# Rotary embedding on one core: the first tile loaded in pieces of two, two and four rows, the sine table spread in a PSUM bank of its own, the last tile stored whole

## The chip, the core and the metric

The kernel runs on one core of a Trainium2 chip. The metric is the device time of one execution in microseconds (us); where several runs are given, it is their median. The engines of the core are TensorE (PE in the profile; PEld are its weight loads), VectorE (DVE), ScalarE (ACT), GpSimd (POOL) and SyncE (SP), which issues all transfers here. Sixteen DMA engines move the data between HBM (the chip's large memory) and SBUF (the core's working memory). PSUM is the small memory into which TensorE writes.

## The reference

`x` has 16 batches of 512 positions of 1024 float32 values, that is 16 heads of 64. Each head is cut into two halves of 32, which are rotated with a cosine and a sine of the position:

```
x = x.reshape(batch, seq, num_heads, head_dim)
x1, x2 = x[..., :half_dim], x[..., half_dim:]
cos, sin = cos[None, :, None, :], sin[None, :, None, :]      # 512 x 32 each
rotated = concatenate([x1 * cos - x2 * sin, x1 * sin + x2 * cos], axis=-1)
```

33.55 MB are read and as many are written.

## The kernel before

**Tiles.** Eight tiles `xt` are worked on in turn. A tile holds two batches: each of its 128 partitions has eight consecutive positions ("rows" 0 to 7 of 1024 values, 32 KB together), so a tile has 4 MB. Five buffers (`BUFS`) hold tiles; results are written over the input in the same buffer, and stored from there. Tiles 5, 6 and 7 use the buffers of tiles 0, 1 and 2 again, so their loads wait until the stores of those have landed.

**Order.** The order is written out by hand (`manual_schedule`), and each engine executes its instructions in the program's order. All transfers are issued by SyncE, one behind the other, and run on one queue: the first piece of tile 0 (`FIRST`, rows 0 to 2), the two tables, the rest of tile 0, tiles 1 to 4, four dummy requests of a few rows of the sine table into `spare` (`EXTRA`, L92), which nobody reads, then the stores of tiles 0, 1, 2, the loads of tiles 5, 6, 7 and the stores of tiles 3 to 7. The last tile is stored in two halves (`LAST_OUT`): rows 0 to 3 once they are done, rows 4 to 7 at the end. Each transfer takes the next of eight completion counters in turn, and the issue of a transfer also waits until the one before it on its counter has landed.

**Tables.** The tables come in as 64 partitions. Two matmuls with a 0/1 matrix `spread` copy them to 128 partitions in PSUM: sine at L113, cosine at L114, both into the bank `tab`. VectorE then writes the sine with both signs to SBUF (`sns`: L116, L117) and copies the signs of row 0 back to `tab` as `own_t` (L119), into the place where the sine was.

**Work on a tile.** The rows are treated in three ways:

- Rows 1-2, 4-5 and 6-7 (`PAIRS`): VectorE multiplies a pair by the cosine into the PSUM buffer `pd` (four banks, L141), GpSimd multiplies the swapped halves by the signed sine into an SBUF buffer `b` (L165), VectorE adds the two into `xt` (L189).
- Row 3: GpSimd makes the sine product, VectorE the cosine product into `pe_ps`, TensorE adds the one onto the other (L176), ScalarE copies the sum to `xt` (L181).
- Row 0: VectorE makes both products (`own_ps` at L141, L150), TensorE adds them (L176), ScalarE copies (L209).

Row 0 of the first tile can begin when its piece and the cosine are there; the first product of GpSimd needs `sns` and rows 1 and 2.

Of the kernel before, what the change touches and what calls it, by code (L numbers as in the profile page):

```python
# [8 lines left out]
FP32 = mybir.dt.float32  # L9
# [9 lines left out]

PAIRS = ((1, 2), (4, 5), (6, 7))  # L20

FIRST = (3, 8)
LAST_OUT = (4, 8)

EXTRA = (2, 4, 5, 6)


@with_exitstack
def kernel(
# [14 lines left out]
    P = nc.NUM_PARTITIONS  # L44
    batch, seq, dim = x.shape
    nh = num_heads
    hd = dim // nh
    half = hd // 2
    PB = P // NB
    KK = seq // PB  # L50
# [13 lines left out]
    pd = ctx.enter_context(tc.tile_pool(name="pd", bufs=1, space=bass.MemoryType.PSUM))  # L64
# [5 lines left out]
    def load(t, lo=0, hi=KK):  # L70
        if tiles[t] is None:
            tiles[t] = xp.tile([P, F], FP32, name="xt")
        s = slice(lo * dim, hi * dim)
        nc.sync.dma_start(out=tiles[t][:, s], in_=x_v[t][:, s])  # L74

    def store(t, lo=0, hi=KK):
        s = slice(lo * dim, hi * dim)
        nc.sync.dma_start(out=out_v[t][:, s], in_=tiles[t][:, s])

    load(0, 0, FIRST[0])  # L80
    tabs = bp.tile([P, 2 * dim], FP32, name="b")
# [3 lines left out]
    nc.sync.dma_start(out=cos_sb, in_=cos_v)  # L85
    for lo, hi in zip(FIRST, FIRST[1:]):
        load(0, lo, hi)
    for t in range(1, BUFS):
        load(t)
    spare = fixed.tile([16, len(EXTRA), 16], FP32)  # L90
    for i, n in enumerate(EXTRA):
        nc.sync.dma_start(out=spare[:n, i], in_=sin_v[:n, :16])  # L92
# [10 lines left out]
    sns = fixed.tile([P, KK, 2, half], FP32)  # L103
    tab = pfix.tile([P, BANK], FP32)
    cos_t = tab[:, : KK * half]
    sin_t = tab[:, KK * half : 2 * KK * half]
    spread = fixed.tile([PB, P], FP32)
    eye = ident[:PB, :PB]
    nc.vector.tensor_copy(
# [81 lines left out]
    def stores(t):  # L191
        lo = 0
        for hi in LAST_OUT if t == NT - 1 else (KK,):
            store(t, lo, hi)
# [64 lines left out]
```

## Time and profile before

| | |
|---|---|
| median of 6 runs | 162.67 us (162.26 to 162.93) |
| the profiled execution | 162.85 us, of which the span of the engines' work is 161.1 |
| VectorE busy | 136.3 us (85% of the span) |
| GpSimd busy | 127.1 us (79%) |
| TensorE busy | 58.2 us (36%) |
| ScalarE busy | 18.7 us (12%) |
| transfers | 67.25 MB, mean 418 GB/s |

The profile is of one execution. Shares are averages over the span, so stretches of it are looked at one by one: slices of a fortieth of the span, in which a digit is the busy share in tenths, or stretches given in microseconds. `L165` is line 165 of the kernel. A row of the timeline has start, duration, engine, line, operation, output and input, and in brackets how long the engine stood idle before it, and who released it. For a transfer the profile gives the line, the size and the time from issue to landing.

### The profile page before, as it was taken

Reading aid. Unit: us, or ns where it says so; the run is one execution under the profiler, and the core shown is the slowest. Engines: PE = TensorE matmul, PEld = TensorE weight load, DVE = VectorE, ACT = ScalarE, POOL = GpSimd, SP = SyncE. Lnnn points to the kernel's source line nnn. Section 1 sums busy time; section 2 is a strip of 40 time slices with the busy share of each in tenths; the row PEclk is TensorE's granted clock in tenths of the full one; section 3 lists DMA queues with packets and bytes.
Section 4 is the critical chain, followed back from the end, with each engine's and each line's share of the span. In section 5 each row is a group of like instructions: output and inputs, shape, how many; then the busy total and the mean of one; then the engine's idle time right before and its main releaser. Section 6 shows DMA issues by size and latency. Waiting matters only on the chain.

```text
span 161.1 us, 443 instructions
## 1 busy us (share of the span) xinstructions
PE 58.2 (36%) x71; PEld 18.1 (11%) x71; DVE 136.3 (85%) x85; ACT 18.7 (12%) x25; POOL 127.1 (79%) x38
## 2 busy tenths in 40 slices
PE   3132805066404840293109330753057303930000
PEld 0111201021002200130004000300021002200000
DVE  1069969999999999999999999999999999997000
ACT  0002401003100301021100310031003100210000
POOL 1049999999999999988998899989989899830000
PEclk9999965557755585559555855576556855595555
DMA  5999999999999999999999999999999999999993
GB/s 189 397 437 441 439 472 391 399 513 391 399 513 391 391 456 456 391 439 472 393 423 480 391 431 480 391 415 488 399 399 505 399 399 496 407 399 444 415 431 142
DMA packets 2787, 67.25 MB, mean 418 GB/s; under 512 B 354, under 2 KB 482, under 8 KB 482
## 3 DMA queue, kind: packets, MB, share of 16 engines
q1 hardware_dynamic: 2786, 67.24, 97.6%
q14 instruction: 1, 0.01, 0.0%
HBM read 33.69 MB, written 33.55 MB: 417 GB/s over the span
## 4 chain that ended last, share of the span: by engine, by line
DVE 68%; issue 12%; POOL 6%; DMA 4%; PE 1%; SPq 0%; DVEq 0%
DVE xt L189 33%; DVE pd L141 31%; POOL b L165 6%; DMA b<-in_sin_dram 4%; DVE pe_ps L141 3%; PE tab L113 1%; PE tab L114 1%; DVE sns L116 0%; DVE xt L150 0%; DVE own_ps L141 0%; SPq L74 0%; DVE sns L117 0%; DVEq L189 0%
## 5 line engine op out<-in xcount | busy, mean ns | idle before, releaser
L165 POOL TENSOR_TENSOR b<-xt,sns 128x2048 f32<-128x2048 f32 (+1 forms) x32 | 126.4, 3981 | 14.5 <-DVE sns L117 9.0
L189 DVE TENSOR_TENSOR xt<-pd,b 128x2048 f32<-128x2048 f32 x24 | 54.9, 2287 | 2.4 <-POOL b L165 1.6
L141 DVE TENSOR_TENSOR pd<-xt,tab 128x2048 f32<-128x2048 f32 x24 | 55.0, 2291 | 0.2
L176 PE MATMUL own_ps<-xt,ident 128*128 128x512 f32 x32 | 29.8, 1086 | 57.0 <-DVE xt L150 51.3
L176 PE MATMUL pe_ps<-b,ident 128*128 128x512 f32 x32 | 26.5, 926 | 23.5 <-DVE pe_ps L141 23.5
L176 PEld LDWEIGHTS own_ps<-xt,ident 128*128 128x128 f32 x32 | 9.4, 323 | 75.3 <-DVE xt L150 60.5
L209 ACT COPY xt<-own_ps 128x1024 f32<-128x1024 f32 x8 | 8.1, 1013 | 75.9 <-PE own_ps L176 75.9
L181 ACT COPY xt<-pe_ps 128x512 f32<-128x512 f32 x16 | 9.4, 587 | 35.6 <-PE pe_ps L176 35.6
L176 PEld LDWEIGHTS pe_ps<-b,ident 128*128 128x128 f32 x32 | 7.3, 249 | 43.1 <-DVE pe_ps L141 34.7
L141 DVE TENSOR_TENSOR pe_ps<-xt,tab 128x512 f32<-128x512 f32 x16 | 11.0, 686 | 0.0
L141 DVE TENSOR_TENSOR own_ps<-xt,tab 128x1024 f32<-128x1024 f32 x8 | 9.8, 1224 | 0.0
L150 DVE TENSOR_TENSOR xt<-xt,tab 128x1024 f32<-128x1024 f32 x8 | 9.7, 1214 | 0.0
L116 DVE TENSOR_SCALAR sns<-tab 128x256 f32<-128x256 f32 x1 | 0.4, 424 | 8.0 <-PE tab L114 8.0
L209 ACT ACT_TABLE_LOAD x1 | 1.3, 1283 | 15.2 <-DVE xt L150 15.2
L113 PE MATMUL tab<-b,spread 64*128 64x256 f32 x2 | 1.2, 696 | 4.8 <-DMA b<-in_sin_dram 4.8
L101 PE MATMUL own_ps<-zero 128*128 128x512 bf16 x2 | 1.0, 622 | 1.2 <-DVE zero L97 1.2
L113 PEld LDWEIGHTS tab<-b,spread 64*128 64x128 f32 x2 | 0.5, 306 | 5.7 <-issue 5.7
L114 PE MATMUL tab<-b,spread 64*128 64x256 f32 x2 | 1.1, 631 | 0.0
L97 DVE MEMSET zero<- 128x256 uint32 x1 | 0.3, 272 | 0.9 <-PEq L240 0.9
L114 PEld LDWEIGHTS tab<-b,spread 64*128 64x128 f32 x2 | 0.7, 333 | 0.2
L101 PE MATMUL pe_ps<-zero 128*128 128x512 bf16 x1 | 0.6, 634 | 0.0
L101 PEld LDWEIGHTS <-zero 128*128 128x128 bf16 x3 | 0.3, 125 | 1.5 <-DVE zero L97 1.2
(9 smaller groups left out, 1.8 us busy)
## 6 DMA issues: line engine op xcount, KB each, us to landing
xt<-in_x_dram SPq DMA_DIRECT2D x7, 4096.0 KB, 29.5
out_dram<-xt SPq DMA_DIRECT2D x7, 4096.0 KB, 24.8
out_dram<-xt SPq DMA_DIRECT2D x2, 2048.0 KB, 11.1
xt<-in_x_dram SPq DMA_DIRECT2D x1, 2560.0 KB
xt<-in_x_dram SPq DMA_DIRECT2D x1, 1536.0 KB
b<-in_sin_dram SPq DMA_DIRECT2D x1, 64.0 KB
b<-in_cos_dram SPq DMA_DIRECT2D x1, 64.0 KB
spare<-in_sin_dram SPq DMA_DIRECT2D x1, 0.1 KB
```

The costliest lines, as they stand in the source:

```text
L97: nc.vector.memset(zero, 0.0)
L101: nc.tensor.matmul(out=ps, lhsT=zero[:, :P], rhs=zero, start=True, stop=True)
L113: nc.tensor.matmul(out=sin_t, lhsT=spread, rhs=sin_sb, start=True, stop=True)
L114: nc.tensor.matmul(out=cos_t, lhsT=spread, rhs=cos_sb, start=True, stop=True)
L116: nc.vector.tensor_scalar_mul(out=sns[:, :, 0, :], in0=sin_k, scalar1=-1.0)
L141: nc.vector.tensor_tensor(out=o, in0=i, in1=cb, op=ALU.mult)
L150: nc.vector.tensor_tensor(out=heads(r), in0=heads(r), in1=s, op=ALU.mult)
L165: nc.gpsimd.tensor_tensor(out=o, in0=i, in1=sb, op=ALU.mult)
L176: nc.tensor.matmul(out=ps, lhsT=ident, rhs=other, start=False, stop=True, skip_group_check=True)
L181: nc.scalar.copy(out=r, in_=pe_ps)
L189: nc.vector.tensor_tensor(out=r, in0=ps, in1=b, op=ALU.add)
L209: nc.scalar.copy(out=r0, in_=own_ps)
```

## The change

Tile 0 is loaded in three pieces (rows 0-1, then behind the tables rows 2-3 and rows 4-7). The last tile is stored in one transfer, behind its last sum. The four dummy requests have one row each. The spread sine goes into the first bank of the `pd` buffer, so that `tab` holds the cosine and `own_t` alone. The instructions of TensorE, ScalarE, GpSimd and VectorE are the same in kind, number and order; SyncE issues one load more and one store less.

```diff
-FIRST = (3, 8)
-LAST_OUT = (4, 8)
-
-EXTRA = (2, 4, 5, 6)
+FIRST = (2, 4, 8)
+LAST_OUT = (8,)
+
+EXTRA = (1, 1, 1, 1)
...
     tab = pfix.tile([P, BANK], FP32)
     cos_t = tab[:, : KK * half]
-    sin_t = tab[:, KK * half : 2 * KK * half]
+    sin_t = pd.tile([P, 2 * dim], FP32, name="pd")[:, : KK * half]
```

## The prediction

> **What bounds the kernel now.** I read the page's 40 slices first, then the table of stretches, the chain, the DMA issues, the waits, and last the single DMA packets of the trace. The slices:
>
> ```profile
> DVE  1069969999999999999999999999999999997000
> ...
> DMA  5999999999999999999999999999999999999993
> ```
>
> A slice is 4.03 us. VectorE (DVE) is full until slice 36 and then stops; the DMA engines are full from slice 1 to slice 38 and go on after VectorE has ended. The stretches say it in numbers:
>
> ```profile
> core 0: us, PE busy (x) PEld busy (x) DVE busy (x) ACT busy (x) POOL busy (x), PEclk, DMA share, GB/s
> ...
> 8.00:148.00 140.00, 56.22 (x68) 17.35 (x66) 135.77 (x83) 18.68 (x25) 126.43 (x32) 0.63 1.01 433
> 148.00:158.50 10.50, 0.00 (x0) 0.00 (x0) 0.00 (x1) 0.00 (x0) 0.00 (x0) 0.50 0.93 399
> ```
>
> The column before the last is the DMA engines' busy share: 1.01 for 140 us (packets overlap a little), at 433 GB/s, and no compute engine works after 148.0. The chain of waits names VectorE for 68%, but it follows one chain only and can't show that the transfers had no idle time either:
>
> ```profile
> DVE 68%; issue 12%; POOL 6%; DMA 4%; PE 1%; SPq 0%; DVEq 0%
> ```
>
> So two resources run full side by side. Which one sets the end is read from the packets. I put them into 16 chains, one per DMA engine (each packet begins within about 30 ns of another's end). In each chain all transfers lie in the order of issue, back to back, from 2.0-2.8 us on: a 32 KB packet takes 1.213 us, a 16 KB one 0.611, so about 9 ns per packet are fixed. Fifteen chains end at 158.54 to 159.15, one at 160.14, and the span ends 0.93 later, at 161.07. Tile 6's store leaves the chains at 148.81 to 149.40, and at 150.41 in the late one. The last half store, issued at 148.0, starts moving only at 153.7, when the half before it is through. VectorE's end at 148.0 is therefore early by over 5 us; **the DMA engines are the bound**, and their work is 67.24 MB plus losses (busy time per engine 157.2 of 161.1 us).
>
> The late chain: at 80.1 a packet of the instruction queue takes its engine for 0.31 us, the next packet is 0.40 too long, and at the change from loads to stores near 109 it loses 0.56, as the last one still loading. The profile page has that packet as its second queue:
>
> ```profile
> q1 hardware_dynamic: 2786, 67.24, 97.6%
> q14 instruction: 1, 0.01, 0.0%
> ```
>
> **The change, part by part.**
>
> *Start.* Rows 0-2 (12 KB per partition) come ahead of the tables now; rows 0-1 (8 KB) will. Eight packets per chain get 4 KB shorter, 8 x (0.460 - 0.309) = 1.2 us, where 0.309 is worked out from the two durations above. The tables' wait is in these rows:
>
> ```profile
> 7.43 1.19 PE L113 MATMUL tab<-b,spread 64*128 64x256 f32 x2 [4.78 <-DMA b<-in_sin_dram]
> ...
> 8.42 1.06 PE L114 MATMUL tab<-b,spread 64*128 64x256 f32 x2
> 9.51 0.42 DVE L116 TENSOR_SCALAR sns<-tab 128x256 f32<-128x256 f32 x1 [7.95 <-PE tab L114]
> ...
> 10.35 22.56 POOL L165 TENSOR_TENSOR b<-xt,sns 128x2048 f32<-128x2048 f32 x6 [9.04 <-DVE sns L117]
> ```
>
> L113 moves from 7.43 to 6.2. *The bank:* L116 waits for L114 although it reads only what L113 wrote, since both lie in one bank. In the pair-product buffer it waits for L113 alone: it starts at 7.4 instead of 9.51. L117 follows by 0.34, L119 (which writes into the cosine's bank and so gains a wait for L114, over at 8.3) starts at 8.3, and `own_ps` L141 at 8.6 instead of 10.56: 2.0 earlier. The buffer's next writer, the first pair product, stands behind L116 and L117 on VectorE, so sharing it costs nothing. But that product and GpSimd's first L165 now need the second piece, rows 2-3. It follows the tables (0.37 us in the chains) and takes 8 x 0.309 plus the 0.21 that the first packet behind the tables loses today: in the chains by 8.2, seen at 8.6-8.8 (after tile 5's load the waiter went on 0.35 later, after sin's 0.6). So L165 starts at 8.7 instead of 10.35: **1.65 earlier**. Its first three operations (4.52 + 2.36 + 4.52) set the second L189, which idles 1.57 for them today; that L189 moves by the same 1.65. Rows 4-7 are there at 13.6, needed at 15.5.
>
> *Middle.* VectorE then runs 1.65 ahead. Does it meet a load? Only tile 5's is near: its last packet ends at 91.74, and
>
> ```profile
> POOL b L165 <- DMA xt<-in_x_dram: 0.8, 1, 0.8
> ```
>
> GpSimd waits for it 0.8 today and would wait 2.45, starting at 92.09 as before and ending its first product at 96.6. VectorE needs that at 101.38 - 1.65 = 99.7; its own first use of tile 5, at 94.59 - 1.65 = 92.9, also lies behind 92.05. The cover is 0.9 us and 3.1 us, so VectorE would end at 148.0 - 1.65 = 146.35. On SyncE the sequence keeps its order: load 5 still stands behind store 2, store 3 behind load 7, which waits for store 2 to land (82.0). All stores but the last are issued 7 us or more before the chains reach them. One more load shifts the completion counters by one: tile 4's load waits for rows 0-1 (seen by about 6), with 38 us of loads queued ahead of it. The dummy requests behind it are covered the same way.
>
> *The dummies.* 17 one-row packets, 11 ns each at about 52 us on six chains, become four requests of one row. On one chain that is what it is now, to within 0.1; split over all chains it adds four packets and four counters at 9-11 ns, 0.08. At worst they break a chain as the tables do (0.21). I take 0 and keep -0.1 to +0.2.
>
> *Pieces.* One more load piece adds 8 packets and a counter per chain, 9 x 9 ns = 0.08; whether its first packet loses 0.21 is bounded by the rows 0.03 (tile 1's load behind the first tile) and 0.21 (behind the tables). The whole last store takes 0.08 away.
>
> *The last store.* Half of it can be issued at 145.38 today; all of it would be issued at 146.35. From issue to first packet the start shows 0.73 to 1.98, 1.25 us, so it stands ready at 147.6, and the first chain asks for it at 148.81: no idle time, 1.2 us of cover. Behind it SyncE has nothing but the end.
>
> The Trainium skill, "DMA: Bandwidth & Descriptors", section "Anatomy of one DMA", gives a DMA about 2.0 us plus its bytes over 436 GB/s (fitted for GpSimd's queue), and "Rules for kernel authors" says to issue early. By that, the whole store would land 11.6 us after VectorE's end instead of the half's 6.8, and the change would lose 4.8 - 1.65, about 3 us. The trace speaks against it:
>
> ```profile
> out_dram<-xt SPq DMA_DIRECT2D x1, 2048.0 KB, 12.2
> ```
>
> That is the half issued at 148.0: 12.2 us to landing for a transfer of 4.9, since over 5 us are queue. The early half only queues.
>
> **Sum.** Chains: +0.08 - 0.08 + 0 (dummies), first and last packets as before; late chain 160.14, span 161.1, plus the 1.75 outside the span: 162.85, the profiled execution's time, which lies 0.18 above the median. Against the median: **162.7**, no change. About 0.2% (0.33 us) is what a measurement of this kernel can tell from none.
>
> **Rivals.**
>
> 1. *The late chain is less late: faster.* The instruction packet belongs to code that the engines reach in their own time; 1.65 us earlier it meets another packet or another engine, and the 0.56 at the change to stores, which hit only the late one so hard, may go too. For it: the chain has 1.0 us over the next (159.15), and six runs differ by 0.67 us, so such losses vary. Against it: the same packet on the same engine costs the same one packet earlier. All of it gone gives 161.7, half 162.2.
>
> 2. *The last store starves the chains: slower.* Place: behind tile 6's store. Idle time begins when VectorE ends after 148.81 - 1.25 = 147.55. The end moves once a chain that restarts passes 160.14: 8 x 1.21 = 9.7 us of packets and 0 to 0.8 for a cold start (what the first packets of the run lost) mean a first packet after 149.6-150.4, a VectorE end after 148.4-149.2. From there each us costs one. It takes the 1.65 lost and 0.4 or more besides, say GpSimd held by tile 5's load and passing it on: at 149.5, 163.0 to 163.9. In runs whose late chain is less late the point lies up to 0.6 earlier. Against it: 3.1 us of cover there. To this side I also count the +0.4 of dummies and piece boundary together, 163.1.
>
> 3. *VectorE is the bound after all: faster by the start's gain.* The chain view suggests it: 162.67 - 1.65 = 161.0. The packets exclude it: 157.2 us of transfers, starting at 2.0, can't end by 158.5. I give it no share of its own.
>
> **Numbers.** No change 0.42; faster (rival 1, around 162.1) 0.32; slower (rival 2 and the added losses, around 163.2) 0.26. No change alone holds 162.35 to 163.0. The range takes in most of both others: 161.8 to 163.3.
>
> **What would show it.** Right: L165 starts near 8.7, VectorE ends near 146.4, the wait for tile 5's load grows to about 2.4, the DMA slices stay at 9 through slice 38, and the store issued near 146.4 takes 13 us or more to land. Wrong: a DMA slice below 9 between 36 and 38 (rival 2), or full slices with a shorter last one and a late chain that ends near 159 (rival 1). A span below 160 would break the whole reading.

## The result: slower by half a per cent

| | median | runs | range |
|---|---|---|---|
| before | 162.52 us | 38 | 162.25 to 162.95 |
| changed | 163.37 us | 17 | 162.73 to 164.35 |

The ratio is 1.0053, with a 95% interval of 1.0042 to 1.0065. The changed kernel is slower, by 0.85 us, and its runs spread over 1.6 us where those of before spread over 0.7. The forecast was no change, 162.7, with a range up to 163.3: the direction was missed, and the time lies just above the range.

The profiled execution of the changed kernel took 162.83 us. It is one of its quickest and as quick as the profiled execution of before (162.85), so its profile shows what the change does at both ends, but none of the loss: where that arises has to be read from the profiles of other kernels. Its slices, VectorE and the DMA engines:

```profile
DVE  1199699999999999999999999999999999994000
...
DMA  5999999999999999999999999999999999999993
```

VectorE stops earlier (slice 36 is 4 instead of 7 tenths), and the DMA engines are as full as before, to the same slice. The stretches of the span (the column before the last is the DMA share) say the same, and that the share holds behind VectorE's end:

```profile
core 0: us, PE busy (x) PEld busy (x) DVE busy (x) ACT busy (x) POOL busy (x), PEclk, DMA share, GB/s
8.00:147.00 139.00, 55.97 (x65) 18.25 (x64) 135.46 (x83) 18.52 (x25) 126.39 (x32) 0.64 1.01 432
147.00:158.50 11.50, 0.00 (x0) 0.00 (x0) 0.00 (x0) 0.00 (x0) 0.00 (x0) 0.50 0.98 425
```

The timeline at the start (start, duration, engine, line, operation; in brackets the idle time before it and its releaser):

```profile
6.37 1.19 PE L113 MATMUL pd<-b,spread 64*128 64x256 f32 x2 [3.72 <-DMA b<-in_sin_dram]
...
7.59 0.42 DVE L116 TENSOR_SCALAR sns<-pd 128x256 f32<-128x256 f32 x1 [6.04 <-PE pd L113]
...
9.00 11.30 POOL L165 TENSOR_TENSOR b<-xt,sns 128x2048 f32<-128x2048 f32 x3 [7.69 <-DMA xt<-in_x_dram]
```

The sine is there 1.1 us earlier, L116 waits for L113 alone and starts 1.9 us earlier, and GpSimd's first product, which now waits for rows 2-3, 1.35 us earlier. At the other end stand VectorE's last sum, SyncE's last issue and that store's time to landing:

```profile
144.35 2.29 DVE L189 TENSOR_TENSOR xt<-pd,b 128x2048 f32<-128x2048 f32 x1
146.71 0.33 SPq L78 DMA_DIRECT2D out_dram<-xt  x1
```

```profile
out_dram<-xt SPq DMA_DIRECT2D x1, 4096.0 KB, 13.3
```

The last sum of before:

```profile
145.71 2.29 DVE L189 TENSOR_TENSOR xt<-pd,b 128x2048 f32<-128x2048 f32 x1
```

VectorE is done 1.36 us earlier than before (146.64 against 148.00), and the whole store takes 13.3 us for 9.7 us of packets: it still queues. All that the change was to do at both ends, it did. The loss is somewhere else.

### The profile page after: what moved, and what is told of

It is laid out like the page before. It is cut to its first block, busy times and chain, and to the rows that moved or that the text cites. A ratio compares the mean times of both kernels' runs of the same rounds, so it can differ in the third digit from the quotient of the medians.

```text
span 160.9 us, 447 instructions
## 1 busy us (share of the span) xinstructions
PE 59.1 (37%) x71; PEld 19.7 (12%) x71; DVE 136.4 (85%) x85; ACT 18.5 (12%) x25; POOL 127.1 (79%) x38
## 4 chain that ended last, share of the span: by engine, by line
DVE 66%; issue 16%; DMA 4%; POOL 3%; SPq 1%; DVEq 0%; POOLq 0%
DVE xt L189 33%; DVE pd L141 29%; DMA xt<-in_x_dram 4%; DVE pe_ps L141 4%; POOL b L165 3%; DVE own_ps L141 0%; SPq L85 0%; SPq L84 0%; DVE xt L150 0%; SPq L74 0%; DVEq L189 0%; POOLq L165 0%
## 5 line engine op out<-in xcount | busy, mean ns | idle before, releaser
L165 POOL TENSOR_TENSOR b<-xt,sns 128x2048 f32<-128x2048 f32 (+1 forms) x32 | 126.4, 3977 | 13.2 <-DMA xt<-in_x_dram 9.9
L176 PE MATMUL pe_ps<-b,ident 128*128 128x512 f32 x32 | 27.0, 938 | 26.9 <-DVE pe_ps L141 26.9
L176 PEld LDWEIGHTS pe_ps<-b,ident 128*128 128x128 f32 x32 | 8.9, 307 | 43.4 <-DVE pe_ps L141 34.8
L116 DVE TENSOR_SCALAR sns<-pd 128x256 f32<-128x256 f32 x1 | 0.4, 425 | 6.0 <-PE pd L113 6.0
L209 ACT ACT_TABLE_LOAD x1 | 1.3, 1283 | 13.3 <-DVE xt L150 13.3
L113 PE MATMUL pd<-b,spread 64*128 64x256 f32 x2 | 1.2, 696 | 3.7 <-DMA b<-in_sin_dram 3.7
L113 PEld LDWEIGHTS pd<-b,spread 64*128 64x128 f32 x2 | 0.5, 306 | 4.6 <-issue 4.6
L114 PE MATMUL tab<-b,spread 64*128 64x256 f32 x2 | 1.1, 631 | 0.0
L114 PEld LDWEIGHTS tab<-b,spread 64*128 64x128 f32 x2 | 0.7, 333 | 0.2
```

What stands on the lines that cost most here:

```text
L113: nc.tensor.matmul(out=sin_t, lhsT=spread, rhs=sin_sb, start=True, stop=True)
L114: nc.tensor.matmul(out=cos_t, lhsT=spread, rhs=cos_sb, start=True, stop=True)
L116: nc.vector.tensor_scalar_mul(out=sns[:, :, 0, :], in0=sin_k, scalar1=-1.0)
L165: nc.gpsimd.tensor_tensor(out=o, in0=i, in1=sb, op=ALU.mult)
L176: nc.tensor.matmul(out=ps, lhsT=ident, rhs=other, start=False, stop=True, skip_group_check=True)
L209: nc.scalar.copy(out=r0, in_=own_ps)
```

## The experiments

### Each part alone

Four kernels make one part of the change each, on the kernel before.

```diff
p_first                          p_last
-FIRST = (3, 8)                  -LAST_OUT = (4, 8)
+FIRST = (2, 4, 8)               +LAST_OUT = (8,)
p_extra                          p_bank
-EXTRA = (2, 4, 5, 6)            -    sin_t = tab[:, KK * half : 2 * KK * half]
+EXTRA = (1, 1, 1, 1)            +    sin_t = pd.tile([P, 2 * dim], FP32, name="pd")[:, : KK * half]
```

> Only the pieces of tile 0 change (2, 2 and 4 rows); dummies, bank and last store stay as before. Theory A (the pieces: an 8 KB piece behind the tables starts slower and lets the sixteen DMA chains drift apart, and the ones that are late lose again at the change from loads to stores): ratio near 1.005, and in the trace the first packets behind the tables lose 0.37 us instead of 0.21 and some chain loses 0.6 us or more at the end of tile 4's load. Theory B (the whole last store): ratio 1.000. Theory C (the dummies): 1.000, with losses at tile 4's load of 0.4 us at most.

> Only the last store changes: whole, behind the last sum. Theory B: VectorE ends at 148.0 as before, the store is issued there and reaches the engines at 149.3, which the earliest chains (148.8) wait for; ratio 1.002 to 1.005. Theories A and C: the latest chain has work until 150.4 in any case, ratio 1.000.

> Only the dummy requests change: four of one row. Theory C (the one-row dummies all on one chain leave the change from loads to stores without the small packets that six chains had): ratio near 1.005 and losses at the end of tile 4's load of up to 0.8 us as in the changed kernel. Theories A and B: ratio 1.000.

> Only the bank of the spread sine changes. VectorE starts about 0.9 us earlier (8.6 instead of 9.51) and ends as much earlier, at about 147; the transfers are the same. All theories: ratio 1.000 (0.998 to 1.002). A ratio near 1.005 would mean that VectorE's earlier course itself costs, say by moving the instruction packet.

| kernel | ratio | 95% interval |
|---|---|---|
| p_first | 1.0050 | 1.0027 to 1.0073 |
| p_last | 0.9995 | 0.9985 to 1.0005 |
| p_extra | 0.9992 | 0.9980 to 1.0004 |
| p_bank | 1.0003 | 0.9991 to 1.0016 |

The pieces of the first tile carry the whole loss. The whole last store, the dummies and the bank are each worth nothing that can be measured. In p_bank L116 started at 9.11 and not at the 8.6 expected: the sine also came later in that execution (L113 at 7.88, not 7.43).

What follows uses times of single packets. Here, as in the prediction and the expectations, they are counted from a point 0.23 to 0.24 us ahead of the zero of the profile's views: the first packet of the kernel before, at 1.98 on this count, begins at 1.74 in the views, and the last one, at 160.14, ends at 159.90. Differences between packets are not touched by this. Where a packet is set against a row of a view, the time on the views' count is given too.

p_last is of use beside that table. SyncE's last issue there, in its timeline:

```profile
148.35 0.33 SPq L78 DMA_DIRECT2D out_dram<-xt  x1
```

That is late enough for the chains to run dry: 0.2 us per chain on average, by the packets. Fifteen chains end at 159.18 to 159.46, where those of before end at 158.54 to 159.15 (the rest of the difference was lost at tile 7's load); the last one, which has the instruction packet, ends at 160.54. Idle time on fifteen chains costs nothing as long as a sixteenth is later, as the prediction had it under its second rival.

p_first shows the opposite. Its stretches at the end (the last two columns are the DMA share and GB/s):

```profile
158.00:159.00 1.00, 0.00 (x0) 0.00 (x0) 0.00 (x0) 0.00 (x0) 0.00 (x0) 0.50 0.73 311
159.00:160.00 1.00, 0.00 (x0) 0.00 (x0) 0.00 (x0) 0.00 (x0) 0.00 (x0) 0.50 0.15 66
```

and those of before:

```profile
158.00:159.00 1.00, 0.00 (x0) 0.00 (x0) 0.00 (x0) 0.00 (x0) 0.00 (x0) 0.50 0.28 115
159.00:160.00 1.00, 0.00 (x0) 0.00 (x0) 0.00 (x0) 0.00 (x0) 0.00 (x0) 0.50 0.04 16
```

A packet is counted here in the stretch in which it begins. Both tails are thin, a few engines finishing alone; that of p_first is thicker and longer, 0.73 + 0.15 against 0.28 + 0.04 us per engine.

### What the chains show

Since the packets carry the answer, I read them in all kernels in the same way. The DMA engines run each load and store of x as eight packets per chain (a table as four) and close it with a packet of 4 bytes. Sorted by time, sixteen such packets in a row give the ends of the sixteen chains for one piece or tile, without having to know which is which. "Late" is the latest of the sixteen against their median. "Lost" is what the packets of tile 4's load and tile 0's store took above 1.213 us (those with over 0.06 too much), added over all chains. Each row is one profiled execution:

```
            tables   late after  late after     lost at the   latest
            start    tile 0      tile 0's       first change  chain
            at, us   loaded, us  store, us      to stores, us ends, us
before       6.32      0.16        0.26            2.5         160.14
p_last       6.34      0.30        0.28            0.6         160.54
p_extra      6.33      0.26        0.35            4.0         159.92
p_bank       6.25      0.35        0.34            0.1         160.04
p_first      5.00      0.93        1.31            8.8         160.69
changed      4.97      0.32        0.89            4.7         159.96
```

With the tables at 5.0 us, one or several chains fall behind, in two places. The first is at the tables: in p_first five of the 128 table packets, which take 0.046 us each, take 0.10 to 0.23, some chains stand still for 0.2 us or more, and three chains are 0.6 to 0.9 us behind the median when tile 0 is in. The second is at 49 to 52 us, about where the first chains go over from tile 4's load to tile 0's store (at 52.2 in p_first): the last packets of the load take up to 0.73 us too long there. Most of them are still on their way when the first chain is through with the load, but 7 of 23 in p_first and 11 of 26 in r_28 (below) have ended by then, so that others store at the same time can't be the whole reason. In the changed kernel's profile most of the lateness comes from this second place (0.23 us before tile 4's load, 0.99 behind it).

### Which property of the pieces

The pieces differ from those of before in three ways: one more piece, a first piece of two rows (which brings the tables to 5.0 us), and nine transfers ahead of the dummies, so that tile 4's load waits on a completion counter.

```diff
r_28     -FIRST = (3, 8)     +FIRST = (2, 8)
r_358    -FIRST = (3, 8)     +FIRST = (3, 5, 8)
r_lane   (pieces of before; one dummy ahead of tile 4's load)
+        if t == BUFS - 1:
+            nc.sync.dma_start(out=lane[:1], in_=sin_v[:1, :16])
         load(t)
r_tabs   (pieces of 2, 2 and 4 rows)
-    load(0, 0, FIRST[0])
     tabs = bp.tile([P, 2 * dim], FP32, name="b")
...
     nc.sync.dma_start(out=cos_sb, in_=cos_v)
+    load(0, 0, FIRST[0])
```

> Two pieces, the first of two rows (rows 0-1, tables, rows 2-7), all else as before. Theory A1 (the third piece and its boundary let the chains drift): ratio 1.000. Theory A2 (an 8 KB first piece brings the tables so early that some chains stall at them): ratio near 1.005, a chain 0.35 to 0.9 us behind the median at the end of tile 0. Theory A3 (nine transfers ahead of the dummies make tile 4's load wait for the first piece and be issued late): 1.000, as there are eight.

> Three pieces, the first of three rows as before (rows 0-2, tables, rows 3-4, rows 5-7). A1: ratio near 1.005. A2: 1.000, the latest chain at most 0.2 to 0.3 us behind the median at the end of tile 0. A3: near 1.005, since tile 4's load is the ninth transfer here.

> The pieces of before, and one dummy request of one row between the loads of tiles 3 and 4, so that tile 4's load is the ninth transfer and waits for the first piece (issued near 7.0 instead of 4.6 us). A3: ratio near 1.005. A1 and A2: 1.000.

> Pieces of two, two and four rows, but both tables ahead of the first piece instead of behind it. A2: no chain meets the tables in the middle of a load; the spread at the end of tile 0 falls to 0.3 us and the ratio to 1.000 or, if the start-up loss of the first packets falls on the tables, a little below. A1 and A3: near 1.005.

| kernel | ratio | 95% interval |
|---|---|---|
| r_28 | 1.0062 | 1.0041 to 1.0084 |
| r_358 | 1.0005 | 0.9993 to 1.0017 |
| r_lane | 0.9999 | 0.9984 to 1.0014 |
| r_tabs | 1.0093 | 1.0074 to 1.0113 |

```
            tables   late after  late after     lost at the   latest
            start    tile 0      tile 0's       first change  chain
            at, us   loaded, us  store, us      to stores, us ends, us
r_358        6.27      0.29        0.28            0.4         160.08
r_lane       6.30      0.44        0.31            2.1         159.70
r_28         4.93      0.74        0.99           10.2         160.73
r_tabs       2.29      0.24        0.50           12.0         161.64
```

A third piece costs nothing (r_358), and neither does the late issue of tile 4's load (r_lane, r_358): A1 and A3 fall. The first piece of two rows stays.

But r_28 can't be counted for A2 by its time, because it has a second loss, which its expectation had missed. Rows 1 and 2 lie in different pieces there, and the second piece is 24 KB per partition long. The waits of r_28:

```profile
POOL b L165 <- DMA xt<-in_x_dram: 12.8, 1, 12.8
...
DVE pd L141 <- DMA xt<-in_x_dram: 3.4, 1, 3.4
```

GpSimd's first product starts at 14.07, VectorE runs late to the end, and the first half of the last tile is issued at 149.65 instead of 145.38. The issues of the last tile's halves, with the time to landing:

```profile
149.65 2.42 SPq L78 DMA_DIRECT2D out_dram<-xt  x2
```

```profile
out_dram<-xt SPq DMA_DIRECT2D x2, 2048.0 KB, 7.7
```

The same row of before:

```profile
out_dram<-xt SPq DMA_DIRECT2D x2, 2048.0 KB, 11.1
```

The halves of r_28 find no queue. Tile 6's store has left the median chain at 149.3 and the latest at 150.3, the first packet behind it begins at 150.72 (150.48 in the views, 0.83 us after the issue), and the chains stand idle for 1.2 us on average. All chains end within 0.2 us of each other at 160.5 to 160.7, 1.8 us behind the median of before. That is the prediction's second rival at work, in another kernel; in the changed kernel it isn't.

r_tabs was expected at 1.000 and is the slowest. With the tables first, the cold start falls on small packets: 31 of the 128 take 0.06 to 0.29 us, x starts at 3.43 instead of 1.98, and the median chain has tile 0 at 14.04 instead of 13.13. The 0.9 us never come back. And the loss at the change to stores is the largest of all, although no chain was late before it.

### Small pieces, early tables or a busy queue

```diff
q_first  (the changed kernel)
-FIRST = (2, 4, 8)
+FIRST = (3, 8)
s_mid    (the changed kernel, last store in halves)
+    load(0, FIRST[0], FIRST[1])
     nc.sync.dma_start(out=sin_sb, in_=sin_v)
     nc.sync.dma_start(out=cos_sb, in_=cos_v)
-    for lo, hi in zip(FIRST, FIRST[1:]):
-        load(0, lo, hi)
+    load(0, FIRST[1], FIRST[2])
s_quiet  (before, with pieces of 2, 2 and 4 rows)
-    for t in range(1, BUFS):
-        load(t)
     spare = fixed.tile([16, len(EXTRA), 16], FP32)
     for i, n in enumerate(EXTRA):
         nc.sync.dma_start(out=spare[:n, i], in_=sin_v[:n, :16])
+    for t in range(1, BUFS):
+        load(t)
```

> The changed kernel with the first tile in the two pieces of before (rows 0-2, tables, rows 3-7); bank, dummies and whole last store as changed. If the first piece alone carries the loss: ratio 1.000 (0.998 to 1.002), VectorE ends about 0.9 us earlier than before (147.1) and the whole store, issued then, still finds the chains at work. If the parts of the change add to each other (the whole store costs once VectorE gains nothing from the pieces): 1.002 to 1.005, with idle time of the chains before the last store.

> Before with pieces of two, two and four rows, the dummies moved ahead of the load of tile 1, so that the loads of tiles 1 to 4 are issued only from about 6 us on, each behind the landing of an earlier transfer. Theory D (the small table packets stall because the queue is still being filled with the descriptors of tiles 1 to 4 when they come at 5 us; at 6.3 that is over): no table packet over 0.06 us, the latest chain at most 0.3 us behind the median after tile 0, ratio 1.000. Theory E (the tables follow a first piece of 8 KB per partition too soon after the cold start, or such pieces read unevenly, whatever is issued): spread 0.35 to 0.9 us and ratio near 1.005 as with the pieces alone.

> The changed kernel with the tables behind the second piece (rows 0-1, rows 2-3, tables, rows 4-7) and the last store in halves as before. The tables reach the chains at about 7.5 us instead of 5.0; VectorE starts about 0.5 us later than before and ends near 148.4. If small pieces as such spread the chains: ratio near 1.005. If it is the early tables (theories D and E's cold start): spread after tile 0 at most 0.3 us and ratio 1.000 to 1.002.

| kernel | ratio | 95% interval | tables start | late after tile 0 | late after tile 0's store | lost at the change | latest chain ends |
|---|---|---|---|---|---|---|---|
| q_first | 0.9993 | 0.9982 to 1.0004 | 6.27 | 0.29 | 0.29 | 0.0 | 159.48 |
| s_mid | 1.0005 | 0.9993 to 1.0017 | 7.39 | 0.12 | 0.33 | 3.3 | 159.63 |
| s_quiet | 1.0036 | 1.0021 to 1.0050 | 5.00 | 0.72 | 1.43 | 6.5 | 161.22 |

s_mid has the same three pieces and the same order of rows as the changed kernel, and its tables have only moved behind the second piece. It loses nothing, so 8 KB pieces as such are harmless, and **the tables at 5 us are what costs**. (The last store in halves, its other difference, is worth nothing by p_last.) That the engines also start earlier behind early tables isn't the reason: in r_28, with the tables at 4.93, GpSimd starts 3.7 us later than before, and the chains fall behind all the same. Its timeline shows the price on the compute side, TensorE at 8.59 instead of 6.37, which the transfers hide:

```profile
8.59 1.19 PE L113 MATMUL pd<-b,spread 64*128 64x256 f32 x2 [5.95 <-DMA b<-in_sin_dram]
```

q_first, the changed kernel without its pieces, is level with the kernel before: the parts don't add to each other. It is the best version that came out, and no better than before within the interval.

s_quiet speaks against theory D. With nothing of tiles 1 to 4 issued before 6.4 us, one table packet still took 0.18 us and one packet behind the tables 0.85 instead of about 0.5, a chain was 0.7 us late after tile 0 and 1.4 after the change to stores, and the ratio is within the interval of p_first's. The slowest table packet took 0.18 to 0.30 us in s_quiet, p_first and r_28, and 0.10 in the changed kernel's quick execution; where the tables come at 6.2 us or later it took 0.10 at most. Why they stall at 5 to 6 us and hardly at 6.3 or 7.4 us is not settled.

### Is lateness itself the price

Two extra reads of 8 KB make one chain late by hand: behind the tables, or only behind tile 7's load, the last load of all.

```diff
+    late = fixed.tile([1, 2, 2 * dim], FP32)
+    for i in range(2):
+        nc.sync.dma_start(out=late[:, i], in_=x_v[0][:1, : 2 * dim])
     for lo, hi in zip(FIRST, FIRST[1:]):     # t_late; t_after has them behind load(n) in stores()
```

> Before, with two extra one-row reads of 8 KB each (0.31 us a packet) behind the tables, into a buffer nobody reads; by the one-row dummies of the changed kernel each should be one packet on one chain, so that one chain is 0.6 to 0.8 us late after tile 0 and nothing else changes. Theory F (a chain that is late when the others turn from loads to stores loses as much again at tile 4's load and at tile 7's): that chain is 1.0 us or more behind after tile 4's load and ratio 1.003 to 1.006. Theory G (lateness only adds): it ends at 158.8 + 0.7 = 159.5, behind which the chain with the instruction packet (160.1) hides it unless they are the same: ratio 1.000 to 1.001. If the reads are split over all chains, none is late and the ratio is 1.000.

> The same two reads, but issued behind tile 7's load, where no change from loads to stores follows for that chain that it could be late for. F: the chain is 0.6 to 0.8 us later from tile 3's store on and loses nothing more; it ends near 159.5, ratio 1.000 to 1.001 (1.004 in runs where it is also the one with the instruction packet). G: the same as t_late.

t_late: 1.0021 (1.0008 to 1.0034). t_after: 1.0008 (0.9994 to 1.0021). Each read is one packet on one chain, in t_late at 6.99 (0.58 us) and 7.57 (0.34 us), in t_after at 110.4 (0.31 us each). In t_late that chain is 0.78 us late after tile 0, 0.96 after tile 0's store and 1.05 at the end: the change to stores took 0.2 us more from it, tile 7's load another 0.1. In t_after two chains end 0.63 and 0.69 us behind the median, and nothing is added.

So a late chain is paid a second time at the changes from loads to stores, but only by a third here; theory F had expected as much again. One chain that is late from the start costs 0.2%, less than half of the change's loss. The difference between the two kernels, 0.0013, is as large as the half-width of either interval, so the runs alone do not separate F from G; the packets do, in one execution of each.

What the early tables add beyond that is that several chains are late at once, and that the loss at the first change to stores is larger: 4.7 to 12.0 us over all chains in the five kernels whose tables come by 5 us, 0 to 4.0 in all those whose tables come later (t_late 3.5). The two ranges nearly touch, and each kernel stands there with one execution. In r_tabs and in the changed kernel's profile that loss is there although no chain was far behind. By what way an early event at 5 us makes packets at 50 us longer stays open.

## Why the prediction was wrong

**Right.** That the transfers are the bound: four kernels that move VectorE's end between 146.6 and 148.3 (changed, p_bank, p_last, q_first) differ only where the chains differ. L116 near 7.4 was 7.59; L165 near 8.7 was 9.00; VectorE's end at 146.35 was 146.64; GpSimd's wait for tile 5's load, foreseen at 2.45, was 9.9 - 7.7 = 2.2 us:

```profile
POOL b L165 <- DMA xt<-in_x_dram: 9.9, 2, 7.7
```

The whole store took 13.3 us to land (13 or more foreseen), and the trace's answer to the rule on issue early was right: p_last, where the store was even issued at 148.35, lost nothing.

**Wrong.** The step that failed is the sum of the chains: "+0.08 - 0.08 + 0 (dummies), first and last packets as before; late chain 160.14". Beside the one late chain that it knew from the instruction packet, it took the sixteen chains to be alike and to stay so, and asked for a new piece only what it adds to each of them. The price of the piece was bounded by rows of the run before, 0.03 to 0.21 us, as a loss common to all chains. Such common losses are there and hardly matter (p_bank lost about 0.45 us on most chains behind the tables, and its ratio is 1.0003). What matters is the one chain that is last, and the run before had no row for that: its table packets, which came at 6.3, all took 0.046 us. Moving the tables to 5.0 us was counted as a gain for VectorE alone, and at nothing for the chains. In the four kernels that have them there behind an 8 KB piece, the latest chain is 0.3 to 0.9 us behind the median after tile 0, and 0.9 to 1.4 after the first store. It shows at once in the changed kernel: rows 2-3, expected through the chains by 8.2, had left the median chain at 8.36 and the latest at 8.71.

Two of its readings set packets against rows and are off by the 0.24 us between the counts: from the first issue to the first packet it is 1.01 us, not 1.25, and the span ends 1.16 us after the last packet, not 0.93. In its sums the two counts cancel, and 157.2 us of transfers from 1.74 on still end behind 158.5, so the forecast doesn't hang on this.

The runs' spread over 0.7 us was put down to the instruction packet; I read it as a chance of a gain (rival 1) and not as a sign that the latest chain can also get later. The Trainium skill, "DMA: Bandwidth & Descriptors", section "Why a DMA increments its semaphore by 16 and not by 1", says that the engines of one transfer finish independently and that only the full count means landed. The trace agrees: in p_first the first and the last of sixteen ends of one store lie 1.6 us apart. That sentence would have asked for the latest engine instead of the mean.

**Rivals.** Rival 1 (the late chain less late) did not come: the instruction packet was there again, at 76.4 us, on a chain that was not the latest. Rival 2 (the store starves the chains) did not come in the changed kernel, but r_28 shows it at its price: first half issued at 149.65, all engines idle for a while, the median chain 1.8 us later. The loss fell into the slower case only by its remainder, the "+0.4 of dummies and piece boundary together": right in sign and near in size, 163.1 against 163.37, but by luck: the dummies cost nothing (p_extra), nor does one more piece boundary (r_358), and the tables' time is not among its reasons.

## What to carry to other kernels

In a kernel that is bound by transfers, the time is that of the latest DMA engine, so look at when each of the sixteen ends a transfer and not only at the busy share, which hardly differs between these profiles. Don't let small transfers into the first microseconds of a stream that must run full: here two tables of 64 KB cost nothing behind 1.5 MB, and half a per cent behind 1 MB. A faster start for a compute engine that isn't the bound gives nothing back, and may be paid for by the one that is.

## What the runs showed of the hardware

- The engines hardly level out. Each has its fixed share of every large transfer, eight packets, and the latest chain, 0.78 us late after tile 0, is still 0.77 us late 30 us later (t_late, tiles 0 to 3); in p_first 0.93 falls to 0.85, in the changed kernel 0.32 to 0.22.
- The last load packets before a change to stores can take longer: up to 0.85 us over their 1.213 (r_tabs, tile 4's load). Most, but not all, are still running when the first engine is through with its loads; the reason is not shown.
- An instruction packet of 0.31 us costs its chain about 0.7: the packet behind it takes 1.61 instead of 1.213 us in the run before.
- Read first of all, 1 KB packets take 0.06 to 0.29 us (31 of 128 in r_tabs); behind 1.5 MB of x nearly all take 0.046 (0.096 at worst, in p_bank).
